# A two-layer decoder trunk: later convolution sums in the statistics bank, SiLU ordered behind the last exponential, state-space products as two of 64 stationary columns

## The chip, the cores and the metric

The kernel runs on one core of a Trainium2 chip, as a single launch. A core has five engines that matter here: TensorE (PE in the profile; its weight loads are shown apart as PEld), VectorE (DVE), ScalarE (ACT), GpSimd (POOL), and SyncE (SP), which only issues transfers. Each engine runs its own instructions strictly in its own order, and they wait for one another through semaphores. The metric is the device time of one execution in microseconds (us). The kernel before took 1105.08 us as the median of three runs (1103.52 to 1105.93).

## The reference, cut to what matters

The input is 512 positions of 1,024 channels, in float32. Two layers follow each other, each a mixer and then a gated feed-forward network (FFN), all with a residual add. The parts that the change touches are in the mixers:

```python
def conv_attn_mixer(xn, ...):                      # layer 0
    h = xn @ w_in
    glu_a, glu_g, c_q, c_kv, k_r = jnp.split(h, SPLIT_EVEN, axis=-1)
    u = glu_a * jax.nn.sigmoid(glu_g)              # 512 channels
    u = causal_dwconv(u, conv_w, conv_b)           # 31 taps, each channel alone
    u = jax.nn.silu(layer_norm(u, conv_ln_g, conv_ln_b))
    ...                                            # q, k, v of 8 heads from c_q, c_kv, k_r
    p = jax.nn.softmax(scores, axis=-1)            # blocks of 128 queries, causal
    attn = jnp.einsum('bhqk,bkhd->bqhd', p, v)     # 64 values per head
    return jnp.concatenate([u, attn], axis=-1) @ w_out

def s5_mixer(xn, ...):                             # layer 1
    u = (xn @ w_in).reshape(b, s, 32, 16)          # 32 groups of 16 channels
    bu = u projected on 64 complex states per group
    x = associative_scan(lam, bu)                  # complex diagonal recurrence in time
    y = Re(C x) + d_skip * u
    z = gelu(y) @ w_glu + b_glu
    return z[..., :1024] * jax.nn.sigmoid(z[..., 1024:])
```

The FFN is `silu(conv3(x @ w_up)[:2816]) * conv3(x @ w_up)[2816:]`, and then `@ w_down`. A last RMSNorm closes the trunk.

## The kernel before, in words

**Layout.** Channels lie on the 128 partitions and the 512 positions are the moving columns. A dense product is made of matmuls with a 128x128 stationary block and 512 moving columns. Weights and inputs are split into a rounded part and a remainder (`whi`, `wlo`; `xh`, `xl`), so that each dense product is three fast matmuls: the rounded weights come from a cast on ACT (L119), their remainders from subtractions on POOL (L121). Products that are left in plain float32 (scores, transposes, the values, the state-space tables) are matmuls without such a split.

**PSUM.** There are eight banks of 128x512, in four tags: three `sc`, two `pt`, two `b`, one `st`. `st` is for statistics (column means, sums of squares, their spreading over partitions).

**Layer 0.** After the input projection come the GLU, then two streams that are interleaved. The causal convolution has four blocks of 128 channels (`conv_gen`, L401 on): a block's sum `acc` stands in a PSUM bank of tag `pt`; DVE adds 20 or so taps to it (L405), while POOL adds the last 10, 10, 11 and 11 taps of the blocks into a sum of its own (L397), from products that ACT makes (L396). At the end ACT copies and DVE adds both into `ycv` (L411, L412), and the bank is free. The attention runs over 32 units (8 heads by 4 query blocks of 128). A unit's score (L553, and the mask added by L554) goes to an `sc` bank, DVE takes the row maximum (L556), ACT the exponential with its sum (L558), DVE the reciprocal (L559), POOL scales the row (L560); TensorE transposes it in 1 to 4 blocks into a `pt` bank (L567), and ACT copies that to SBUF (L570, `prob`). There are six buffers for scaled rows, and six units lie between a score and its transposes in the program. After each second head TensorE multiplies with the values (L583, two heads as two column halves of 64 in a `b` bank); ACT and DVE split the result (L587, L588). Behind the attention stands the LayerNorm of the convolution: mean (L615), squares (L620), `stat` and `spread`, scaling on DVE (L627), SiLU on ACT (L628), cast on ACT (L630) and remainder on POOL (L631). Both halves go into the output projection `wo` (L104), which is added to `x` (L648).

**FFN of layer 0.** While it starts, DVE and POOL also make the tables of the state-space layer from small vectors (from L763 on); a MEMSET of `pr` starts that chain, in memory that the convolution's pool leaves when the last POOL remainder (L631) is done. The norm of the FFN's input (`xh` L267, `xl` L268) and the FFN's own elementwise work (L922, L925, L937) are on the same DVE queue.

**Layer 1.** The state-space mixer works on four sets q of 8 groups each. A step `E` multiplies the set's inputs with table E (`e`, 8 products of a 128x128 table and 64 moving columns), and DVE runs the recurrence on it (`xs`); a step `T` multiplies the inputs with table T into bank `y`, a step `O` adds the states times table O, and then a GELU and two transfers give the input of the output projection `gl`. A string sets the order of these by hand, and TensorE's instructions are held to it (`D` is a number of dense matmuls, a number behind a comma how many dense matmuls are laid between the products of a step, `t` a load of tables):

```python
PLAN = "D39 t1 E0,12 t2 E1,8 D10 T0 O0 t3 E2 T1 O1 E3 T3 T2 A1 O2,6 D12 O3"
```

**What sets the order.** Outside of this string and of the convolution's taps, which are held in program order, a list scheduler places the instructions on each engine from its own estimates of when operands and buffers are ready. ACT needs a table of functions for exponentials and another for SiLU; it loads one (`ACT_TABLE_LOAD`) wherever two neighbours in its order differ.

Of the kernel before, what the change touches and what calls it, by code (L numbers as in the profile page):

```python
# [13 lines left out]
AF = mybir.ActivationFunctionType  # L14
# [20 lines left out]
NC = T // CL  # L35
# [36 lines left out]
def trunk(ctx, tc, A, out):  # L72
# [14 lines left out]
    def bank(name, tag=None):  # L87
        if tag is None:
            tag = CYCLE[turn[0] % len(CYCLE)]
            turn[0] += 1  # L90
        return pp.tile([128, T], F32, tag=tag, bufs=TAGS[tag], name=name)
# [6 lines left out]


    held = tc.keep_in_program_order  # L100
    fixed = [False]

    def mm(*a, **kw):
# [58 lines left out]
    def col(name, i=0):  # L162
        return vec[:, VOFF[name] + i:VOFF[name] + i + 1]
# [186 lines left out]
    with tc.tile_pool(name="l0", bufs=1) as lp:  # L350
# [12 lines left out]
        y, ysum = {}, []  # L363
# [34 lines left out]
                yield  # L398

        def conv_gen(i, u):  # L400
            acc = bank("acc", "pt")  # L401
            s.activation(acc, u, AF.Identity, scale=col("cw", i * CK + CK - 1), bias=col("cb", i))
            first = CK - POOL_TAPS[i]
            for sh in range(1, first):
                held(v.scalar_tensor_tensor(acc[:, sh:], u[:, :T - sh], col("cw", i * CK + CK - 1 - sh),  # L405
                                           acc[:, sh:], ALU.mult, ALU.add))
                yield
            while len(pools) and pools[0][0] <= i:
                pool_taps(1)
            y[i] = ya = lp.tile([128, T], F32, tag="acc", bufs=4, name="ycv")  # L410
            s.copy(ya[:, :first], acc[:, :first])  # L411
            v.tensor_tensor(ya[:, first:], acc[:, first:], psum_[i][:, first:], ALU.add)  # L412
            if i == 1:
                ysum.append(lp.tile([128, T], F32, tag="ysum", name="ysum"))
                v.tensor_tensor(ysum[0], y[0], y[1], ALU.add)
            elif i > 1:
                v.tensor_tensor(ysum[0], ysum[0], y[i], ALU.add)
# [121 lines left out]
        def head_q(h):  # L539
# [5 lines left out]
            v.tensor_tensor(q, ps, tO if h % 2 else tE, ALU.mult)  # L545
            return q

        def score(qi, qk):
            q, k = qk
            L = 128 * (qi + 1)  # L550
            sl = slice(qi * 128, L)
            ps = bank("sc", "sc")
            pe.matmul(ps[:, :L], q[:, sl], k[:, :L], start=True, stop=False)  # L553
            pe.matmul(ps[:, sl], identb, maskb, start=False, stop=True)  # L554
            mx = lp.tile([128, 4], F32, tag="mx", bufs=6, name="mx")
            v.reduce_max(mx[:, 0:1], ps[:, :L], axis=mybir.AxisListType.X, negate=True)  # L556
            p = lp.tile([128, T], F32, tag="p", bufs=6, name="p")
            s.activation(p[:, :L], ps[:, :L], AF.Exp, bias=mx[:, 0:1], accum_out=mx[:, 1:2])  # L558
            v.reciprocal(mx[:, 2:3], mx[:, 1:2])  # L559
            g.tensor_scalar(p[:, :L], p[:, :L], mx[:, 2:3], 1.0, ALU.mult, ALU.mult)  # L560
            return p
# [63 lines left out]
        rl = spread(rowstat((sqs, CW, LN_EPS))[0], two=True)  # L625
        for i in range(4):
            v.tensor_tensor(y[i], y[i], rl, ALU.mult)  # L627
            s.activation(y[i], y[i], AF.Silu, scale=col("ln_g", i), bias=col("ln_b", i))  # L628
            h, l = xhi(), xlo()
            s.copy(h, y[i])  # L630
            g.tensor_tensor(l, y[i], h.bitcast(F32), ALU.subtract)  # L631
            mix[4 + i] = (h, l)
# [328 lines left out]
    tTs, tOs = [], []  # L961
# [26 lines left out]

    xs, ys = {}, []

    def s5_state(q, d):
        gq = slice(8 * q, 8 * q + 8)
        cf, sf = (t[:, gq].rearrange("p g c -> p (g c)") for t in (tC, tS))
        e1 = bank("e1", "sc" if q < 3 else "b")
        for i in gaps(d):
            mm(e1[:, i * NC:(i + 1) * NC], tE[:, 8 * q + i], rs[q][:, i], start=True, stop=True)
        za, zb, z = ztmp("za"), ztmp("zb"), ztmp("z")
        lo, hi = slice(0, 64), slice(64, 128)

        def swapped(dst, src, low):  # L1000
            v.tensor_tensor(dst[lo], src[hi], sf[hi], ALU.mult)
            g.tensor_tensor(dst[hi], low[lo], sf[lo], ALU.mult)

        s.copy(z[lo], e1[lo])
        v.tensor_tensor(za, e1, cf, ALU.mult)
        swapped(zb, e1, z)
        v.tensor_tensor(za, za, zb, ALU.subtract)
        v.tensor_tensor_scan(z, tD[:, gq].rearrange("p g c -> p (g c)"), za, 0.0, ALU.mult, ALU.add)
        x_, xb = ztmp("xs"), ztmp("xb")
        xs[q] = as_g(x_)  # L1010
        g.memset(xs[q][:, :, 0:1], 0.0)
        v.tensor_tensor(za, z, cf, ALU.mult)
        swapped(xb, z, z)
        v.tensor_tensor(xs[q][:, :, 1:], as_g(za)[:, :, :NC - 1], as_g(xb)[:, :, :NC - 1], ALU.add)
# [3 lines left out]
    def s5_direct(q, d):  # L1018
        y = yb[q] = bank("y", "pt")
        for i in gaps(d):  # L1020
            mm(y[:, i * NC:(i + 1) * NC], tTs[q][:, i], rs[q][:, i], start=(i == 0), stop=False)

    def s5_out(q, d):
        y = yb[q]
        for i in gaps(d):
            mm(y[:, i * NC:(i + 1) * NC], tOs[q][:, i], xs[q][:, i], start=False, stop=(i == 7))
        ya = tmp("ya")
        s.activation(ya, y, AF.Gelu_apprx_tanh)
        dy = dp.tile([CL, 128, NC], F32, tag=f"dy{q}", name=f"dy{q}")
# [264 lines left out]
```

## Time and profile before

| | before |
|---|---|
| median of three runs | 1105.08 us |
| profiled execution | 1104.31 us, its span 1102.5 us |
| mean granted TensorE clock | 0.965 |
| TensorE busy | 1046.9 us (95%) |
| VectorE, ScalarE, GpSimd busy | 657.1, 454.0, 681.0 us |
| convolution taps and attention | about 100 to 190 us in the span |
| output projection `wo` | 175 to 226 us |
| FFN of layer 0 | from 226 us |
| state-space products | 640 to 687 us |

The times in the rows that follow are microseconds from the start of the span. A row of the timeline has the start, the busy time, the engine, the line and operation, the tile written and the tiles read, shapes, the number of instructions drawn together, and in square brackets how long the engine had been idle before it and what ended that. A row of the table by windows has, behind the window and its length, the busy time and number of instructions of PE, PEld, DVE, ACT and POOL, then the granted TensorE clock (1.00 is full), the share of the DMA engines and the GB/s. One float32 product of TensorE is recorded as two matmuls. The ends of matmuls are modelled, so lengths are read from one start to the next.

### The profile page before, as it was taken

The page shows a single profiled execution, that of the slowest core. Times are in us where ns is not written, and L with a number is a line of the kernel's source. Part 1 is how long each engine was busy: PE and PEld are TensorE (multiplying, and loading weights), DVE is VectorE, ACT ScalarE, POOL GpSimd, SP SyncE. Part 2 cuts the span into 40 slices and gives each one's busy share as a digit, 9 for nine tenths or more (in the row PEclk, how much of TensorE's full clock was granted, in tenths as well). Part 3 has the DMA queues.
Part 4 walks back from the last instruction along what each step waited for, and adds up shares of the span by engine and source line. Part 5 has one row for each costly group of instructions (what it writes and reads, how often), then busy time and mean ns, then how long its engine had stood idle before and what let it go on. Part 6 is the DMA issues. An engine that isn't in the chain of part 4 may idle for free.

```text
span 1102.5 us, 13795 instructions
## 1 busy us (share of the span) xinstructions
PE 1046.9 (95%) x4774; PEld 848.8 (77%) x4774; DVE 657.1 (60%) x1271; ACT 454.0 (41%) x669; POOL 681.0 (62%) x827
## 2 busy tenths in 40 slices
PE   7998698979999999999999799999999999999996
PEld 5875355857788878888888689788888888888896
DVE  7768871899865778547765465567531344314445
ACT  5567575341552253422444222544432344224441
POOL 4898841655677686766765652567656566556660
PEclk9999798989999999999999886999999999999998
DMA  5423010412233333333333552223223322232322
GB/s 189 144 68 90 14 40 1 130 64 91 78 114 113 116 104 110 115 103 109 97 101 110 210 153 60 91 84 110 98 93 107 102 98 96 77 115 96 101 73 77
DMA packets 54597, 108.64 MB, mean 99 GB/s; under 512 B 20608, under 2 KB 28416, under 8 KB 54528
## 3 DMA queue, kind: packets, MB, share of 16 engines
q1 hardware_dynamic: 54528, 107.77, 30.7%
q8 instruction: 38, 0.62, 0.2%
q14 instruction: 31, 0.25, 0.1%
HBM read 98.31 MB, written 8.39 MB: 97 GB/s over the span
## 4 chain that ended last, share of the span: by engine, by line
PE 77%; DVE 11%; ACT 5%; POOL 3%; issue 2%; DMA 2%; SPq 0%; DVEq 0%; ACTq 0%; POOLq 0%
PE dn L104 22%; PE ug L104 20%; PE ua L104 20%; PE gl L104 4%; POOL wlo L121 2%; PE y L104 2%; PE pv L583 1%; PE wo L104 1%; DVE acc L405 1%; PE w L104 1%; PE sc L553 1%; PE e L104 1%; POOL pa L397 1%; DMA raw<-w 1%; PE q L104 1%
## 5 line engine op out<-in xcount | busy, mean ns | idle before, releaser
L121 POOL TENSOR_TENSOR wlo<-raw,whi 128x256 fp32r<-128x256 f32 x639 | 486.2, 793 | 259.2 <-ACT whi L119 218.0
L119 ACT CAST whi<-raw 128x1024 fp32r<-128x1024 f32 (+1 forms) x162 | 167.2, 1037 | 303.1 <-PE dn L104 91.5
L104 PE MATMUL dn<-ghl,whi 128*128 128x512 f32 (+1 forms) x632 | 192.9, 387 | 0.0
L104 PE MATMUL ug<-xh,whi 128*128 128x512 f32 x352 | 138.6, 394 | 3.9 <-DVE wi L708 3.9
L104 PE MATMUL ua<-xl,whi 128*128 128x512 f32 x352 | 137.6, 391 | 4.2 <-DVE xl L268 4.2
L104 PE MATMUL ua<-xh,whi 128*128 128x512 f32 x352 | 138.0, 392 | 1.9 <-ACT xh L267 1.9
L104 PE MATMUL ug<-xh,wlo 128*128 128x512 f32 x352 | 138.2, 392 | 0.0
L104 PE MATMUL ug<-xl,whi 128*128 128x512 f32 x352 | 137.8, 392 | 0.0
L104 PE MATMUL ua<-xh,wlo 128*128 128x512 f32 x352 | 137.6, 391 | 0.0
L104 PEld LDWEIGHTS dn<-ghl,whi 128*128 128x128 f32 x632 | 117.3, 188 | 24.5 <-issue 0.8
L104 PE MATMUL dn<-ghl,wlo 128*128 128x512 f32 (+1 forms) x316 | 121.8, 386 | 0.0
L949 DVE TENSOR_TENSOR x<-x,dn 128x512 f32<-128x512 f32 x40 | 26.8, 683 | 110.0 <-PE dn L104 110.0
L925 DVE SCALAR_TENSOR_TENSOR ug<-h,vec,ug 128x511 f32<-128x511 f32 x88 | 66.3, 753 | 43.2 <-ACT ug L923 41.9
L925 DVE SCALAR_TENSOR_TENSOR ua<-h,vec,ua 128x511 f32<-128x511 f32 x88 | 66.3, 753 | 41.8 <-ACT ua L923 40.4
L104 PEld LDWEIGHTS ug<-xh,whi 128*128 128x128 f32 x352 | 66.8, 190 | 18.8 <-ACT whi L119 4.7
L104 PEld LDWEIGHTS ua<-xl,whi 128*128 128x128 f32 x352 | 66.3, 188 | 18.4 <-DVE xl L268 4.8
L104 PEld LDWEIGHTS ua<-xh,whi 128*128 128x128 f32 x352 | 66.4, 188 | 16.5 <-ACT xh L267 2.4
L104 PEld LDWEIGHTS ug<-xh,wlo 128*128 128x128 f32 x352 | 66.7, 190 | 14.2 <-POOL wlo L121 0.3
L104 PEld LDWEIGHTS ug<-xl,whi 128*128 128x128 f32 x352 | 66.7, 190 | 13.8
L104 PEld LDWEIGHTS ua<-xh,wlo 128*128 128x128 f32 x352 | 66.3, 188 | 14.0 <-POOL wlo L121 0.3
L941 POOL TENSOR_TENSOR ghl<-g,ghl 128x512 fp32r<-128x512 f32 x44 | 57.0, 1294 | 31.4 <-ACT ghl L940 31.4
L104 PEld LDWEIGHTS dn<-ghl,wlo 128*128 128x128 f32 x316 | 59.4, 188 | 11.8
(343 smaller groups left out, 1836.5 us busy)
## 6 DMA issues: line engine op xcount, KB each, us to landing
raw<-up SPq DMA_DIRECT2D x88, 512.0 KB, 3.3
raw<-down SPq DMA_DIRECT2D x32, 512.0 KB, 3.3
raw<-w SPq DMA_DIRECT2D x14, 512.0 KB, 3.5
raw<-down SPq DMA_DIRECT2D x16, 384.0 KB, 3.1
raw<-wg SPq DMA_DIRECT2D x8, 512.0 KB, 4.1
raw<-wo_a SPq DMA_DIRECT2D x4, 512.0 KB, 3.3
raw<-wo_c SPq DMA_DIRECT2D x4, 512.0 KB, 5.0
park_O<-wn SPq DMA_DIRECT2D x8, 256.0 KB, 2.6
```

Source lines behind the costliest of these rows:

```text
L104: r = pe.matmul(*a, **kw)
L119: s.copy(hi[:, :n], r)
L121: (eng or g).tensor_tensor(lo[:, a:a + 2], r[:, a:a + 2], hi[:, a:a + 2].bitcast(F32), ALU.subtract)
L397: held(g.tensor_tensor(pa[:, sh:], pa[:, sh:], pb[:, sh:], ALU.add))
L405: held(v.scalar_tensor_tensor(acc[:, sh:], u[:, :T - sh], col("cw", i * CK + CK - 1 - sh), acc[:, sh:], ALU.mult, ALU.add))
L553: pe.matmul(ps[:, :L], q[:, sl], k[:, :L], start=True, stop=False)
L583: pe.matmul(ps[a, kt * 128:], vv[:, kt, i * 128 + 64 * e:i * 128 + 64 * e + 64], pts[e][:, 4 * kt:3 * kt + 4].rearrange("p k c -> p (k c)" ...
L925: v.scalar_tensor_tensor(ps[:, sh:], t[:, :T - sh], col(fw, 3 * j + 2 - sh), ps[:, sh:], ALU.mult, ALU.add)
L941: g.tensor_tensor(lo, gt, h.bitcast(F32), ALU.subtract)
L949: v.tensor_tensor(x[m], x[m], ps, ALU.add)
```

## The change

There are three parts. The sums of convolution blocks 2 and 3 stand in the single `st` bank instead of the two `pt` banks, so block 3 begins when block 2 has left it, and the `pt` banks hold transposes alone from then on. The first SiLU is ordered behind the last exponential on ACT, with a dependency that is an order on one engine and no semaphore. Each product with a state-space table (24 per set: `e`, `y` from T, `y` from O) becomes two, with the first and the last 64 columns of the stationary block, written to the first and last 64 partitions of the same bank.

```diff
+    def behind(ins, first):
+        tc.add_manual_dep(ins.ins, first.ins.name, mybir.DependencyInfo(
+            mybir.DependencyClass.NoSync, mybir.DependencyReason.DATA), reason="order on one engine")
 ...
         def conv_gen(i, u):
-            acc = bank("acc", "pt")
+            acc = bank("acc", "pt" if i < 2 else "st")
 ...
+        exps = []
 ...
-            s.activation(p[:, :L], ps[:, :L], AF.Exp, bias=mx[:, 0:1], accum_out=mx[:, 1:2])
+            exps.append(s.activation(p[:, :L], ps[:, :L], AF.Exp, bias=mx[:, 0:1], accum_out=mx[:, 1:2]))
 ...
-            s.activation(y[i], y[i], AF.Silu, scale=col("ln_g", i), bias=col("ln_b", i))
+            silu = s.activation(y[i], y[i], AF.Silu, scale=col("ln_g", i), bias=col("ln_b", i))
+            if i == 0:
+                behind(silu, exps[-1])
 ...
+    def halves(ps, i, w, mv, start, stop):
+        for a in (slice(0, 64), slice(64, 128)):
+            mm(ps[a, i * NC:(i + 1) * NC], w[:, a], mv, start=start, stop=stop)
 ...
-            mm(e1[:, i * NC:(i + 1) * NC], tE[:, 8 * q + i], rs[q][:, i], start=True, stop=True)
+            halves(e1, i, tE[:, 8 * q + i], rs[q][:, i], True, True)
 ...
-            mm(y[:, i * NC:(i + 1) * NC], tTs[q][:, i], rs[q][:, i], start=(i == 0), stop=False)
+            halves(y, i, tTs[q][:, i], rs[q][:, i], i == 0, False)
 ...
-            mm(y[:, i * NC:(i + 1) * NC], tOs[q][:, i], xs[q][:, i], start=False, stop=(i == 7))
+            halves(y, i, tOs[q][:, i], xs[q][:, i], False, i == 7)
```

The scheduler's order moves with it. Line numbers below are those of each kernel: the change adds 5 lines ahead of the matmul helper (L104 becomes L109) and 7 ahead of the scores (L553 becomes L560).

TensorE, at the first transposes of the attention; before, nine scores stand ahead of the first transpose (`sc` is a score or its mask, `pt` a transpose of one block):

```order
L553 MATMUL sc<-kt,q 128x128
L554 LDWEIGHTS identb
L554 MATMUL sc<-maskb,identb 128x128
L567 MATMUL pt<-ident,p 128x128
L553 MATMUL sc<-kt,q 128x256
L554 LDWEIGHTS identb
L554 MATMUL sc<-maskb,identb 128x128
L567 MATMUL pt<-ident,p 128x128 x2
L553 MATMUL sc<-kt,q 128x384
```

The same engine and place in the changed kernel, from its second group of transposes on (the first transpose stands behind four scores):

```order
L560 MATMUL sc<-kt,q 128x128
L561 LDWEIGHTS identb
L561 MATMUL sc<-maskb,identb 128x128
L574 MATMUL pt<-ident,p 128x128 x5
L560 MATMUL sc<-kt,q 128x256
L561 LDWEIGHTS identb
L561 MATMUL sc<-maskb,identb 128x128
L574 MATMUL pt<-ident,p 128x128 x5
L560 MATMUL sc<-kt,q 128x384
```

Where one unit's transposes stood between two scores, those of two units do, since two `pt` banks take them; the column mean of the LayerNorm, which stood among the scores, now stands behind the last score.

ScalarE, around the SiLU of the LayerNorm, before (`p` is the exponential, `prob` the copy of transposes, `ycv` the SiLU in place):

```order
L628 ACT_TABLE_LOAD
L628 ACTIVATE ycv<-ycv,vec 128x512
L558 ACT_TABLE_LOAD
L558 ACTIVATE p,mx<-sc,mx 128x128
L570 COPY prob<-pt 128x3x128
L628 ACT_TABLE_LOAD
L628 ACTIVATE ycv<-ycv,vec 128x512 x3
L570 COPY prob<-pt 128x4x128
L558 ACT_TABLE_LOAD
L558 ACTIVATE p,mx<-sc,mx 128x256
```

And in the changed kernel (`whi` is the cast of a weight block of `wo`):

```order
L577 COPY prob<-pt 128x3x128
L577 COPY prob<-pt 128x4x128
L635 ACT_TABLE_LOAD
L635 ACTIVATE ycv<-ycv,vec 128x512 x2
L594 CAST xh<-pv 128x512
L639 CAST xh<-ycv 128x512
L635 ACTIVATE ycv<-ycv,vec 128x512
L639 CAST xh<-ycv 128x512
L635 ACTIVATE ycv<-ycv,vec 128x512
L639 CAST xh<-ycv 128x512
L124 CAST whi<-raw 128x1024
L639 CAST xh<-ycv 128x512
```

All four SiLUs now stand behind the last copy of transposes, with one table load ahead of them; the cast of a value product and one of weights stand among them. Over the whole kernel ACT's table loads go from 14 to 10.

TensorE, in the step E0, before (`w` is a dense matmul of the state-space input projection, `e` a product with table E):

```order
L104 MATMUL w_5822<-xl,whi 128x512
L104 MATMUL e_5847<-r,tabE 128x64
L104 MATMUL w_5822<-xh,wlo 128x512
L104 MATMUL e_5847<-r,tabE 128x64
L104 MATMUL w_5822<-xh,whi 128x512
```

And in the changed kernel:

```order
L109 MATMUL w_5822<-xl,whi 128x512
L109 MATMUL e_5847<-r,tabE 64x64 x2
L109 MATMUL w_5822<-xh,wlo 128x512
L109 MATMUL e_5847<-r,tabE 64x64 x2
L109 MATMUL w_5822<-xh,whi 128x512
```

The order around the products is the same; each product with a table is now two matmuls of 64 stationary columns, 192 in place of 96.

## The prediction

> **What bounds the kernel now.** I read the page's busy shares and chain first, then TensorE's timeline through the attention and the state-space products, then the other engines there.
>
> ```profile
> PE 1046.9 (95%) x4774; PEld 848.8 (77%) x4774; DVE 657.1 (60%) x1271; ACT 454.0 (41%) x669; POOL 681.0 (62%) x827
> PE 77%; DVE 11%; ACT 5%; POOL 3%; issue 2%; DMA 2%; SPq 0%; DVEq 0%; ACTq 0%; POOLq 0%
> ```
>
> TensorE sets the time. It can win only where it idles, where its clock is down, or where its own work shrinks. The attention has the first two:
>
> ```profile
> 111.01 0.44 PE L553 MATMUL sc<-kt,q 128*128 128x128 f32 x2
> 116.13 0.33 PE L567 MATMUL pt<-ident,p 128*128 128x128 f32 x1 [4.62 <-DVE ycv L412]
> 117.22 1.22 PE L553 MATMUL sc<-kt,q 128*128 128x256 f32 x2 [0.76 <-ACT p L558]
> ...
> 122.79 2.08 PE L553 MATMUL sc<-kt,q 128*128 128x512 f32 x2 [0.55 <-ACT p L558]
> ...
> 138.37 0.38 PE L553 MATMUL sc<-kt,q 128*128 128x128 f32 x2
> ...
> 159.70 0.38 PE L553 MATMUL sc<-kt,q 128*128 128x128 f32 x2
> ...
> 165.91 1.13 PE L553 MATMUL sc<-kt,q 128*128 128x512 f32 x2 [2.10 <-ACT p L558]
> ...
> 170.28 4.51 PE L583 MATMUL pv<-prob,vv 128*64 128x512 f32 x14 [3.07 <-ACT prob L570]
> ...
> 187.69 2.37 PE L583 MATMUL pv<-prob,vv 128*64 128x512 f32 x14
> 189.99 0.50 PE L104 MATMUL wo<-xh,whi 128*128 128x512 f32 x1
> ```
>
> The ninth of 32 scores starts at 111.01. The first transpose then waits 4.62 us for a convolution sum to leave its `pt` bank; both banks hold sums. From 117.22 to 122.79 two units pass, 2.8 us each; from 138.37, with the banks free, twelve units take 21.33 us, 1.78 each. The last score starts at 165.91, the last value product ends by 189.99. The windows show the clock falling with the idle time:
>
> ```profile
> 112.00:131.00 19.00, 12.04 (x30) 6.15 (x31) 16.55 (x31) 11.00 (x26) 16.62 (x17) 0.64 0.06 14
> 131.00:161.00 30.00, 28.35 (x150) 17.73 (x150) 24.21 (x66) 20.54 (x60) 13.97 (x23) 1.00 0.13 41
> 161.00:175.00 14.00, 8.83 (x36) 4.63 (x34) 4.52 (x13) 11.87 (x21) 2.86 (x6) 0.76 0.00 1
> ```
>
> The second hole, 161 to 175, is ACT's: 11.87 of 14 us busy, on copies, exponentials and table loads that alternate with SiLUs. Two of the four loads there:
>
> ```profile
> 166.25 1.28 ACT L628 ACT_TABLE_LOAD   x1
> ...
> 170.25 1.28 ACT L558 ACT_TABLE_LOAD   x1
> ```
>
> **The change, attention.** *Banks.* Transposes no longer wait for sums 2 and 3. From 111.01 I let the 23 other units run at 1.78 us: 40.9 us, so the last score starts near 152 instead of 165.91; I take 153. The work of the others fits, tightly: DVE was busy 16.55 + 24.21 = 40.8 us in the two windows up to 161, and some 7 of them (mean, squares and scaling of the LayerNorm) now stand behind the last score, which leaves 34 in 42 us. The new serial step, block 3's sum behind block 2's in one bank, costs nothing as long as DVE has other work and the mean is needed only behind the last score; if that cover is gone, the LayerNorm is late (third rival).
>
> *SiLU order.* No table load stands between exponentials. From the last score's start to the end of the last value product it was 189.99 - 165.91 = 24.1 us. Out of this fall the wait of 3.07 and the half clock on the product at 170.28 (4.51 against 2.37, so 2.1); the mean (1 us) comes in. 24.1 - 5.2 + 1.0 = 19.9, so 153 + 19.9 = 173, **17 us** earlier than 189.99. Below, the stretch from 138.37 to 159.70 also held LayerNorm matmuls that now stand elsewhere, about 2.5 us by an estimate; without them it is 1.57 per unit, 23 x 0.21 = 5 us less, an end at 168. Above, a quarter of a microsecond more per unit gives 179. That is a gain of 11 to 22.
>
> *What is late next.* The tail of the LayerNorm, and with it a chain on DVE:
>
> ```profile
> 190.58 2.18 ACT L630 CAST xh<-ycv 128x512 fp32r<-128x512 f32 x4
> 194.18 2.00 ACT L119 CAST whi<-raw 128x1024 fp32r<-128x1024 f32 x2 [1.42 <-PE wo L104]
> ```
>
> ```profile
> 191.29 5.05 POOL L631 TENSOR_TENSOR xl<-ycv,xh 128x512 fp32r<-128x512 f32 x4 [14.21 <-ACT xh L630]
> ```
>
> ```profile
> 196.42 0.09 DVE L763 MEMSET pr<- 128x32 f32 x1 [5.00 <-POOL xl L631]
> ...
> 270.65 0.68 DVE L922 TENSOR_TENSOR h<-ua,rb 128x512 f32<-128x512 f32 x1
> ```
>
> ```profile
> 237.86 0.79 PE L104 MATMUL ua<-xl,whi 128*128 128x512 f32 x1 [4.21 <-DVE xl L268]
> 277.46 0.79 PE L104 MATMUL ug<-xh,whi 128*128 128x512 f32 x1 [3.85 <-DVE wi L708]
> ```
>
> DVE starts its state-space tables at 196.42, 6.4 us behind the last value product, and works without a hole until `h` (270.65) empties the first bank of the FFN; TensorE waits for DVE at 237.86 and 277.46. So what lands is DVE's start, not TensorE's. In the changed order ACT's fourth `ycv` cast stands behind a cast of weights, which waits for the first block of `wo` (36 matmuls, as between 174.92 and 189.99, less what else lies there: some 4 us behind the value product), and POOL does four `wlo` pieces (about 0.8 us each, the 5.05 us above being 1.26 for each larger one) ahead of the last `xl`. Start behind the value product: 4.3 + 1.0 + 3.2 + 1.3 = 9.8 us instead of 6.4. DVE begins at 173 + 9.8 = 182.8, **13.6 us** earlier. Seven fewer small table instructions stand ahead of the first `h` in DVE's order; at some 0.27 us each 2 us more. The attention part lands at **-15.6 us**; bounds -22 (end at 168, tail as before) and -3 (third rival).
>
> **The change, state space.**
>
> ```profile
> 650.78 1.89 PE L104 MATMUL y<-r,tabT 128*128 128x64 f32 x16
> ...
> 659.07 3.62 PE L104 MATMUL y<-r,tabT 128*128 128x64 f32 x16
> 662.49 3.62 PE L104 MATMUL y<-xs,tabO 128*128 128x64 f32 x16
> ...
> 676.14 1.06 PE L104 MATMUL y<-xs,tabO 128*128 128x64 f32 x4
> ...
> 685.47 1.89 PE L104 MATMUL y<-xs,tabO 128*128 128x64 f32 x16
> ```
>
> ```profile
> 656.00:683.00 27.00, 27.00 (x120) 26.31 (x120) 20.09 (x21) 5.13 (x7) 9.72 (x9) 0.50 0.28 79
> ```
>
> A product takes (662.49 - 659.07)/8 = 0.427 us at half clock and some 0.225 at full. Weight loads are busy 26.31 of 27 us: the load of 128 float32 columns sets the pace, not the 64 moving columns. Whether two loads of 64 columns run beside each other, only the value products tell:
>
> ```profile
> 152.41 1.02 PE L553 MATMUL sc<-kt,q 128*128 128x512 f32 x2
> 153.27 0.22 PE L554 MATMUL sc<-maskb,identb 128*128 128x128 bf16 x1
> 153.42 2.37 PE L583 MATMUL pv<-prob,vv 128*64 128x512 f32 x14
> ```
>
> ```profile
> 181.19 1.07 PE L583 MATMUL pv<-prob,vv 128*64 128x512 f32 x2
> 182.19 0.50 PE L104 MATMUL wo<-xh,whi 128*128 128x512 f32 x1
> 182.53 0.39 PE L104 MATMUL wo<-xl,whi 128*128 128x512 f32 x1
> ```
>
> A float32 product of 512 columns takes 153.27 - 152.41 = 0.86 us. The 14 records at 187.69 are 2,048 columns in two halves; one after another they would take 3.4 us, and took 2.3. Halves do run beside each other, moving data at least. If loads do so too, a pair takes half a product: 0.213 at half clock. But one half alone, between other work (181.19 to 182.19), took 1.00 instead of 0.86, and the matmul behind it 0.34 instead of 0.23: a visit to the 64-column form costs 0.25 us.
>
> This drain is also a rule of the Trainium skill ("TensorEngine Tiling (Array Packing)", Key Properties: changing the tiling mode drains TensorE, and different tiles load and multiply in parallel); by its second half alone the stage would halve, by its first alone the 16 products of E0 and E1 would lose. The rows show both.
>
> Step by step. E0 and E1 stand between dense matmuls: 16 visits x 0.25 = 4 us more on TensorE; half of this shifts DVE's recurrence (2 us), since TensorE runs ahead of it. From then on DVE counts:
>
> ```profile
> 660.97 0.68 DVE L1014 TENSOR_TENSOR xs<-za,xb 128x504 f32<-128x504 f32 x1
> ...
> 667.52 0.68 DVE L1014 TENSOR_TENSOR xs<-za,xb 128x504 f32<-128x504 f32 x1
> ...
> 677.08 0.68 DVE L1014 TENSOR_TENSOR xs<-za,xb 128x504 f32<-128x504 f32 x1
> ```
>
> One set takes it 6.55 us, so the 40 products from 659.07 to 676.14, which would need 8.5 us instead of 17.1, cannot pass this on whole: `xs` of set 2 is ready at 670.2. Behind it stand O2, 18 dense matmuls (0.23 us each at full clock, 0.43 at half) and six visits: 6.5 to 12.4 us, and `xs` of set 3 comes at about 678.8. O3 starts between 678.8 and 682.6 instead of 685.47, so 3 to 6.7 us earlier; I take **-5 us**. Behind O3 the distance to the last `gl` parts stays. Bounds: -8 (no shift of DVE, clock up) and +5 (loads one after another, 0.45 us for a pair at full clock, next to the visits).
>
> **Sum.** 1104.31 (span 1102.5, 1.8 around it) - 15.6 - 5 = 1083.7; the median lies 0.8 above that execution: **1084 us**.
>
> **The rivals.**
>
> *Both parts pay, as above*: 0.53, about 1084, own range 1074 to 1091.
>
> *The state-space clock comes up too.* At 0.50 for 27 us with TensorE never idle, the rows speak against this; but the halves double the moving columns per time, and the sum would be at its bound, -8: 1081. Chance 0.07. "TensorE: Matmul & The Clock Gate" of the Trainium skill (Part 1) has the clock full after about 3.4 us of sustained work; by that rule alone the window above could not be at half clock, so the trace bears it out only if load-bound work doesn't count.
>
> *Halves don't overlap their loads.* The value products' 14 records have long moving parts that could hide serial loads, so this stands open: 0.225 stays 0.225 plus an issue cost, visits come on top, +5: 1104.31 - 15.6 + 5 + 0.8 = 1094.5. Chance 0.20.
>
> *The attention's gain is swallowed.* If block 3's sum ends so late that mean, squares, spread and SiLU follow far behind the last value product, DVE's tables start hardly earlier. With only 3 us left of 15.6: 1104.31 - 3 - 5 + 0.8 = 1097. For it speaks that POOL was busy 16.62 of 19 us while the taps ran. Chance 0.13, a quarter of it within no change.
>
> *Slower: the pace is not the banks'.* Score, maximum, exponential and scaling pass through DVE and POOL queues full of taps. If 2.8 us per unit is theirs, all 23 units cost 23 x 1.0 = 23.5 us more than I allow, and the result is 1084 + 23.5 = 1107.5. It decides from 1.78 + 21/23 = 2.7 us per unit. Against it: that stretch ran at clock 0.64 beside a single free bank, and DVE's share between 131 and 161, with taps until the mean, was still 24.21 of 30. Chance 0.07.
>
> **How the numbers follow.** A measurement of this kernel tells about 0.2% (2.2 us) from no change. Faster: 0.53 + 0.07 + 0.20 + 0.10 = 0.90; same 0.03; slower 0.07. The range takes the first four cases in: 1074 to 1098.
>
> **What would show it.** No wait for `ycv` ahead of the first transpose; the last value product ending near 173; DVE's MEMSET of `pr` near 183; no table load between exponentials. In layer 1, starts of successive products 0.11 or 0.21 us apart and O3 some 5 us closer to the start of E0. Wrong would be: units more than 2.4 us apart after 112, the MEMSET beyond 190, or products no closer than before.

## The result and the profile after

The changed kernel takes 1072.40 us (median of four runs, 1071.96 to 1073.62) beside 1105.51 us of the kernel before on the same chip (1103.52 to 1106.94): a ratio of 0.9708, with a 95% interval of 0.9687 to 0.9729, or 33 us less. 1084 were forecast, with 1074 to 1098 as the range; the result lies below it. The direction and both stages were right; the gain was half again as large. The profiled execution took 1072.81 us with a span of 1071.0 us, so the two spans differ by 31.5 us.

The page of the changed kernel, its busy shares and the chain:

```profile
PE 1025.4 (96%) x4966; PEld 826.2 (77%) x4966; DVE 660.5 (62%) x1271; ACT 447.5 (42%) x665; POOL 680.1 (63%) x827
...
PE 75%; DVE 15%; ACT 3%; DMA 2%; issue 2%; POOL 2%; SPq 0%; DVEq 0%; POOLq 0%; ACTq 0%
```

TensorE in the attention, from the timeline, and the windows of the same stretch:

```profile
106.57 0.27 PE L574 MATMUL pt<-ident,p 128*128 128x128 f32 x1
...
112.09 0.44 PE L560 MATMUL sc<-kt,q 128*128 128x128 f32 x2
...
148.29 1.08 PE L560 MATMUL sc<-kt,q 128*128 128x512 f32 x2
...
165.87 2.37 PE L590 MATMUL pv<-prob,vv 128*64 128x512 f32 x14
168.17 0.50 PE L109 MATMUL wo<-xh,whi 128*128 128x512 f32 x1
```

```profile
112.00:131.00 19.00, 17.95 (x95) 11.43 (x94) 17.75 (x40) 17.81 (x48) 17.79 (x24) 1.00 0.18 49
131.00:149.00 18.00, 18.00 (x94) 10.72 (x93) 15.54 (x42) 14.77 (x45) 16.15 (x23) 1.00 0.10 32
149.00:169.00 20.00, 20.00 (x104) 13.85 (x103) 12.05 (x33) 10.71 (x22) 2.12 (x3) 1.00 0.00 1
```

The first transpose no longer waits. From the ninth score (112.09) to the last (148.29) 23 units pass in 36.2 us, 1.57 us each; TensorE has work in 56 of the 57 us and the clock stays at 1.00, where it was at 0.64 and 0.76. From the last score's start to the end of the value products it is 168.17 - 148.29 = 19.9 us. They end 21.8 us earlier than before. From the ninth score on the gain is 22.9 us: the end of the value products lay 189.99 - 111.01 = 78.98 us behind it and lies 168.17 - 112.09 = 56.08 us behind it now. The other 1.1 us went in the first 100 us of this execution, where the order is the same and the first score came at 100.52 instead of 97.44. From the ninth score on the traces repeat well: 78.71 and 78.92 us in two further runs with the attention's order of before (halves alone, `nr` behind `xl` on before), 56.1 to 56.2 in all eleven others with the changed one.

What follows, on POOL and DVE, and TensorE's waits in the first FFN:

```profile
176.25 1.31 POOL L640 TENSOR_TENSOR xl<-ycv,xh 128x512 fp32r<-128x512 f32 x1
```

```profile
177.63 0.09 DVE L772 MEMSET pr<- 128x32 f32 x1 [8.05 <-POOL xl L640]
```

```profile
209.83 0.50 PE L109 MATMUL ua<-xl,whi 128*128 128x512 f32 x1 [1.93 <-DVE xl L273]
...
239.09 0.50 PE L109 MATMUL ug<-xh,whi 128*128 128x512 f32 x1 [2.76 <-ACT whi L124]
...
252.05 0.50 PE L109 MATMUL ug<-xh,whi 128*128 128x512 f32 x1 [1.43 <-ACT sl L943]
...
264.76 0.50 PE L109 MATMUL ug<-xh,whi 128*128 128x512 f32 x1 [1.47 <-ACT whi L124]
```

The first down-product (`dn`) of this FFN, before and in the changed kernel:

```profile
328.18 0.62 PE L104 MATMUL dn<-ghl,whi 128*128 128x512 f32 x2
```

```profile
303.30 0.62 PE L109 MATMUL dn<-ghl,whi 128*128 128x512 f32 x2
```

DVE's table work starts 9.5 us behind the last value product (6.4 before), 18.8 us earlier than before. The first down-product is 24.9 us earlier.

In the state-space layer, from the timelines of TensorE and DVE, and one window of the changed kernel, with the window of the kernel before behind it:

```profile
614.92 0.34 PE L109 MATMUL e<-r,tabE 128*64 128x64 f32 x4 [0.22 <-DMA r<-du]
615.19 0.50 PE L109 MATMUL w<-xh,wlo 128*128 128x512 f32 x1
615.62 0.34 PE L109 MATMUL e<-r,tabE 128*64 128x64 f32 x4
...
629.84 1.10 PE L109 MATMUL y<-xs,tabO 128*64 128x64 f32 x32
630.77 1.10 PE L109 MATMUL e<-r,tabE 128*64 128x64 f32 x32
...
638.40 1.98 PE L109 MATMUL y<-xs,tabO 128*64 128x64 f32 x32 [5.59 <-DVE xs L1027]
...
654.17 1.15 PE L109 MATMUL y<-xs,tabO 128*64 128x64 f32 x32 [1.56 <-DVE xs L1027]
```

```profile
637.02 1.33 DVE L1027 TENSOR_TENSOR xs<-za,xb 128x504 f32<-128x504 f32 x1
```

```profile
628.50:656.00 27.50, 19.69 (x343) 16.46 (x343) 24.82 (x24) 8.02 (x11) 13.87 (x13) 0.88 0.33 97
```

```profile
650.50:687.20 36.70, 35.42 (x181) 34.00 (x180) 25.49 (x26) 7.47 (x9) 13.81 (x14) 0.63 0.26 72
```

Eight pairs of halves take 630.77 - 629.84 = 0.93 us, 0.116 us for a product that took 0.225 at full clock and 0.427 at half. The clock in the stage is 0.88, where it was 0.63 over the stage and 0.50 in the 27 us without a gap; TensorE is busy for 19.69 of 27.5 us. TensorE now waits for DVE, 5.59 and 1.56 us. Behind the longer wait the clock is down again (0.50 from 638.4 to 642): eight pairs then take 640.16 - 638.40 = 1.76 us, 0.22 us each. From the last `gl` matmul on the shift is 31.9 us: 24.9 from the first layer and 7.0 from this stage.

### The profile page after: what moved, and what is told of

The parts are those of the page before. It is cut to its first block, busy times and chain, and to the rows that moved or that the text cites. A ratio compares the mean times of both kernels' runs of the same rounds, so it can differ in the third digit from the quotient of the medians.

```text
span 1071.0 us, 14173 instructions
## 1 busy us (share of the span) xinstructions
PE 1025.4 (96%) x4966; PEld 826.2 (77%) x4966; DVE 660.5 (62%) x1271; ACT 447.5 (42%) x665; POOL 680.1 (63%) x827
## 4 chain that ended last, share of the span: by engine, by line
PE 75%; DVE 15%; ACT 3%; DMA 2%; issue 2%; POOL 2%; SPq 0%; DVEq 0%; POOLq 0%; ACTq 0%
PE ug L109 20%; PE dn L109 20%; PE ua L109 20%; PE gl L109 4%; PE win L109 3%; POOL wlo L126 2%; DVE acc L410 2%; PE pv L590 1%; PE wo L109 1%; PE sc L560 1%; PE w L109 1%; PE pt L574 1%; PE kb L907 1%; DMA raw<-w 1%; ACT whi L124 1%
## 5 line engine op out<-in xcount | busy, mean ns | idle before, releaser
L109 PE MATMUL dn<-ghl,whi 128*128 128x512 f32 (+1 forms) x632 | 192.9, 387 | 0.0
L109 PE MATMUL ug<-xh,whi 128*128 128x512 f32 x352 | 138.0, 392 | 5.7 <-ACT whi L124 4.2
L109 PE MATMUL ua<-xl,whi 128*128 128x512 f32 x352 | 137.4, 390 | 1.9 <-DVE xl L273 1.9
L109 PE MATMUL ug<-xh,wlo 128*128 128x512 f32 x352 | 137.9, 392 | 0.2
L109 PE MATMUL ua<-xh,whi 128*128 128x512 f32 x352 | 137.6, 391 | 0.0
L109 PE MATMUL ug<-xl,whi 128*128 128x512 f32 x352 | 137.5, 391 | 0.0
L109 PE MATMUL ua<-xh,wlo 128*128 128x512 f32 x352 | 137.1, 390 | 0.0
L109 PEld LDWEIGHTS dn<-ghl,whi 128*128 128x128 f32 x632 | 117.3, 188 | 24.6 <-issue 0.8
L109 PE MATMUL dn<-ghl,wlo 128*128 128x512 f32 (+1 forms) x316 | 121.8, 386 | 0.0
L934 DVE SCALAR_TENSOR_TENSOR ug<-h,vec,ug 128x511 f32<-128x511 f32 x88 | 66.2, 753 | 42.7 <-ACT ug L932 41.4
L109 PEld LDWEIGHTS ug<-xh,whi 128*128 128x128 f32 x352 | 66.4, 189 | 20.9 <-ACT whi L124 5.1
L109 PEld LDWEIGHTS ua<-xl,whi 128*128 128x128 f32 x352 | 66.3, 188 | 16.0 <-DVE xl L273 2.4
L109 PEld LDWEIGHTS ug<-xh,wlo 128*128 128x128 f32 x352 | 66.2, 188 | 14.7 <-POOL wlo L126 1.1
L109 PEld LDWEIGHTS ua<-xh,whi 128*128 128x128 f32 x352 | 66.1, 188 | 14.2 <-issue 0.6
L109 PEld LDWEIGHTS ug<-xl,whi 128*128 128x128 f32 x352 | 66.3, 188 | 13.7
L109 PEld LDWEIGHTS ua<-xh,wlo 128*128 128x128 f32 x352 | 66.2, 188 | 13.8
L109 PEld LDWEIGHTS dn<-ghl,wlo 128*128 128x128 f32 x316 | 59.4, 188 | 11.7
```

Source lines behind the costliest of these rows:

```text
L109: r = pe.matmul(*a, **kw)
L934: v.scalar_tensor_tensor(ps[:, sh:], t[:, :T - sh], col(fw, 3 * j + 2 - sh), ps[:, sh:], ALU.mult, ALU.add)
```

## The experiments

Below, a shift is that of an instruction in the profiled execution against the same one in the profile before, whose own row shows where the two instructions stand. Each ratio is taken against the kernel before on the same chip and in the same hours; the runs come from several chips, so medians of different hours are compared by their ratios. The shift of the MEMSET of `pr` is DVE's start; "up-products" is the time from the last `wo` matmul to the first down-product of the first FFN, which is the same work for TensorE in every kernel.

| run | median, us | ratio to before (95%) | MEMSET of `pr` | first down-product | up-products |
|---|---|---|---|---|---|
| before | 1104 to 1106 | | 196.42 | 328.18 | 102.9 |
| changed | 1072.40 | 0.9708 (0.9687 to 0.9729) | -18.8 | -24.9 | 99.9 |
| bank alone | 1077.37 | 0.9755 (0.9718 to 0.9792) | -20.1 | -24.6 | 101.5 |
| SiLU alone | 1099.30 | 0.9946 (0.9920 to 0.9972) | -2.5 | -3.1 | 102.4 |
| halves alone | 1098.48 | 0.9943 (0.9928 to 0.9959) | -2.0 | -1.9 | 103.0 |
| whole in E0, E1, O2 | 1071.45 | 0.9701 (0.9666 to 0.9735) | -19.0 | -26.0 | 99.0 |
| changed, again | 1071.44 | 0.9687 (0.9662 to 0.9712) | -19.5 | -25.4 | 100.2 |
| last remainder on DVE | 1076.77 | 0.9744 (0.9725 to 0.9764) | -20.3 | -20.2 | 103.3 |
| block 3 alone in `st` | 1079.02 | 0.9759 (0.9740 to 0.9778) | -19.6 | -19.2 | 103.3 |
| shorter tables | 1071.00 | 0.9688 (0.9670 to 0.9706) | -20.0 | -25.9 | 100.2 |
| E0 and E1 in one run | 1069.00 | 0.9666 (0.9647 to 0.9685) | -20.6 | -27.2 | 99.3 |
| tables behind `xl` | 1078.81 | 0.9758 (0.9741 to 0.9774) | -19.1 | -21.0 | 104.0 |
| tables behind `rb` | 1081.36 | 0.9781 (0.9764 to 0.9798) | -21.8 | -23.9 | 103.9 |
| tables behind `rb`, E0 and E1 in one run | 1078.21 | 0.9746 (0.9724 to 0.9767) | -22.1 | -26.2 | 101.8 |
| `nr` behind `xl`, DVE remainder | 1078.34 | 0.9756 (0.9733 to 0.9778) | -25.2 | -21.6 | 106.9 |
| `nr` behind `xl`, before | 1107.71 | 1.0015 (0.9996 to 1.0035) | -0.3 | +2.7 | 105.9 |
| `pr` behind `xl`, DVE remainder | 1075.85 | 0.9726 (0.9705 to 0.9748) | -24.3 | -23.1 | 104.5 |

### The three parts alone

The bank alone, on the kernel before:

```diff
-            acc = bank("acc", "pt")
+            acc = bank("acc", "pt" if i < 2 else "st")
```

> The kernel before with the sums of blocks 2 and 3 in the statistics bank, nothing else. Its instructions stand on every engine in the same order as with the SiLU ordering added, 10 table loads included, so theory 1 (the bank alone makes the whole attention gain, the ordered SiLU adds nothing) expects what the changed kernel has without its state-space gain of 7.1 us: 24.9 us below before, 1080.6, and the last value product 21.8 us earlier. Theory 2 (the gain needs the ordered SiLU too, as the prediction put it) expects the wait of 3.07 us and the half clock at the last value products to be still there: 5 us less gain, 1085 to 1086.

It measured 1077.37 us, 27 us below the before of its hours (1104.33): theory 1. The last value product is 23.1 us earlier, 22.9 of them from the ninth score on. The order says why the ordered SiLU cannot add anything. In the traces of the bank alone and of the changed kernel TensorE, DVE, ACT and POOL have the same rows in the same order up to the state-space products, table loads included; the LayerNorm's mean stands behind the last score in both, so its SiLUs come behind the last exponential by themselves. The edit is inert in the changed kernel.

The ordered SiLU alone (`behind(silu, exps[-1])` for the first of the four):

> The kernel before with the first SiLU ordered behind the last exponential, nothing else. ACT's order here has 12 table loads instead of 14: the other three SiLUs, which are not ordered, still stand among the exponentials. Theory 1 (the bank is the cause): within 2 us of before, 1103 to 1106, with the wait of 4.62 us for the convolution sum unchanged. Theory 2 (the table loads cost what the second hole shows): 4 to 6 us faster, 1099 to 1101.

1099.30 us, 5.0 below before: the size that theory 2 gave, and theory 1's "within 2 us" was wrong. In its trace TensorE's and POOL's rows stand in the order of before, so that no matmul was moved. The profile shows the first hole untouched and the second one smaller:

```profile
117.30 0.33 PE L573 MATMUL pt<-ident,p 128*128 128x128 f32 x1 [4.63 <-DVE ycv L416]
...
168.23 3.79 PE L589 MATMUL pv<-prob,vv 128*64 128x512 f32 x14 [2.20 <-ACT prob L576]
```

So table loads among the exponentials did cost TensorE time: 3.07 became 2.20 us, 4.51 became 3.79, and the wait of 2.10 ahead of the last score went, 3.7 us in all with two of the four loads gone. But with the bank they go anyway, and the two gains are not two.

The halves alone:

> The kernel before with the state-space products as two of 64 columns, nothing else. Theory 1 (the stages add): 7.1 us below before, 1098.4, a pair of halves 0.12 us apart at full clock, and each product between dense matmuls 0.24 us dearer. Theory 2 (the gain of layer 1 depends on the earlier arrival, through transfers or table work of the first FFN): under 4 us, 1101 or more.

1098.48 us, 5.9 below before; in the traces the stretch from the first down-product to the last `gl` matmul is 5.2 us shorter (394.6 against 399.7 us). Nearer to theory 1, at a gain between the predicted 5 and the 7 of the changed kernel's trace. By the medians the bank's 27.0 us and the halves' 5.9 make 32.9, the 33 of the whole change; with the SiLU's 5.0 they would make 38.

### What bounds the state-space stage now

Whole products wherever dense matmuls lie between them:

```diff
-            halves(e1, i, tE[:, 8 * q + i], rs[q][:, i], True, True)
+            halves(e1, i, tE[:, 8 * q + i], rs[q][:, i], True, True) if not d else mm(e1[:, i * NC:(i + 1) * NC], tE[:, 8 * q + i], rs[q][:, i], start=True, stop=True)
```

(and the same in the O step.)

> The changed kernel, but the products of a step with dense matmuls between them (E0, E1, O2) stay whole, 128 columns; the steps without any keep their halves. Theory 1 (the 16 visits of E0 and E1 cost TensorE 0.24 us each and delay VectorE's recurrence): 2 to 4 us below the changed kernel, 1068.5 to 1070.5, and the wait for xs ahead of the second O step no longer than 5.6 us. Theory 2 (VectorE and GpSimd set this stage, TensorE waits for them anyway): within 1 us of the changed kernel, 1071.5 to 1073.5.

1071.45 us, no different from the changed kernel: theory 2. TensorE gets the visits back and hands them over to a wait:

```profile
636.98 1.97 PE L109 MATMUL y<-xs,tabO 128*64 128x64 f32 x32 [5.93 <-DVE xs L1027]
```

The products of E0 and E1 in one run each:

```diff
-PLAN = "D39 t1 E0,12 t2 E1,8 D10 T0 O0 t3 E2 T1 O1 E3 T3 T2 A1 O2,6 D12 O3"
+PLAN = "D39 t1 E0 D12 t2 E1 D18 T0 O0 t3 E2 T1 O1 E3 T3 T2 A1 O2,6 D12 O3"
```

> The changed kernel with the products of E0 and of E1 in one run each: 12 dense matmuls between the two steps and 18 behind E1, none between products. Theory 1 (VectorE's recurrence sets this stage, and an earlier E0 starts it earlier): no visits of 0.24 us, the recurrence begins some 4 us earlier, 2 to 4 us below the changed kernel's 1071.4. Theory 2 (GpSimd's weight remainders and VectorE's other work fill the stage anyway, as with whole products in E0 and E1): within 1 us.

1069.00 us, the lowest median of the study, with a ratio of 0.9666 where the changed kernel had 0.9708 and 0.9687; the interval overlaps that of the second (0.9647 to 0.9685, 0.9662 to 0.9712). The trace doesn't show a gain in the stage: from the first down-product to the last `gl` matmul it takes 392.1 us, 392.2 and 392.7 in the two profiles of the changed kernel. The 2 us stand in the first layer, which the edit doesn't touch. That fits theory 2. The same edit on the kernel with the tables behind `rb` (below) goes from 1081.36 to 1078.21 us on one chip, with intervals that just overlap; whether it is faster stays open.

### What sets the landing in the first FFN

The changed kernel again, as the reference of this part:

> The changed kernel itself, beside the three that differ from it in one place. All theories: 32 to 33 us below before, 1071 to 1073.

1071.44 us, as expected.

The fourth LayerNorm remainder on DVE instead of POOL:

```diff
-            g.tensor_tensor(l, y[i], h.bitcast(F32), ALU.subtract)
+            (v if i == 3 else g).tensor_tensor(l, y[i], h.bitcast(F32), ALU.subtract)
```

> The changed kernel with the fourth LayerNorm remainder (xl of ycv) on VectorE instead of GpSimd, where it stands behind four weight remainders. VectorE's table work should start 3 us earlier (near 174.6 instead of 177.6). Theory D (VectorE's start sets when the first FFN gets going): 2 to 3 us below the changed kernel. Theory T (TensorE lands by its own work; VectorE's chain only fills its waits): within 1 us of it.

Neither: 1076.77 us, 5.3 slower than the changed kernel of the same hours. DVE's start is 6.7 us behind the end of the value products (169.41 to 176.15) instead of 9.5 (168.17 to 177.63), so nearly 3 us earlier against TensorE, as meant, but the up-products take 103.3 us instead of 100. The scheduler laid the table work differently among the FFN's: the last remainder `xl` of the FFN's norm stands 144 rows of DVE behind the MEMSET of `pr` in this trace, not 118 as in the changed kernel's (138 and 115 in the count of the expectations).

The same position came with block 3's sum alone in `st`:

```diff
-            acc = bank("acc", "pt" if i < 2 else "st")
+            acc = bank("acc", "pt" if i < 3 else "st")
```

> The changed kernel with the sum of block 3 alone in the statistics bank; block 2 goes back to a pt bank, so that it holds one of two while blocks 2 and 3 are summed. If it is the number of free pt banks that sets the pace (theory 1), the units up to the end of block 2 run at a pace between 1.57 and 2.8 us; of the 27 us that the bank alone gave, a third to two thirds is lost: 9 to 18 us above the changed kernel. If one free bank is enough and only the full stop at the first transpose hurt (theory 2): at most 4 us above it.

1079.02 us, 7.6 above the changed kernel: less than theory 1 expected, more than theory 2. From the ninth score on the value products end after 60.7 us instead of 56.1 (79.0 before), and the up-products take 3 us longer. In the attention one free bank keeps the transposes going. Up to the last score (151.33) 5.4 us are lost: 1.0 us is the column mean, which stands among the scores again, and most of the rest lies in the one window whose clock is not full, with a wait of 2.58 us for DVE ahead of a projection:

```profile
112.00:131.00 19.00, 15.97 (x73) 9.88 (x72) 16.70 (x32) 14.28 (x39) 15.65 (x21) 0.91 0.15 41
```

So 18.3 of the 22.9 us come with one bank kept free, and the second bank is worth the smaller part. How much of the 18.3 is the full stop at the first transpose and how much the low clock behind it (0.64), these runs don't separate.

Shorter table work:

```diff
-        for j in range(CL):
-            v.tensor_copy(prr[:, j], pr[:, CL - 1 - j])
-            ts(spir[:, j], pi[:, CL - 1 - j], s1, None, ALU.mult)
+        v.tensor_copy(prr, pr[:, :CL])
+        ts(spir, pi[:, :CL], s1, None, ALU.mult)
```

> The changed kernel with two VectorE instructions in place of sixteen at the start of the table work: the powers are copied without reversing their order, which leaves the reversal out of the computation. Some 3.5 us of VectorE time go, seven instructions fewer stand ahead of the first h. Theory D (VectorE's chain sets the landing): 2 to 4 us below the changed kernel. Theory T (TensorE lands by its own work): within 1 us of it.

This kernel leaves out the reversal of the powers, so it computes other values; the rest of the program is the same. 1071.00 us against 1071.44: theory T. DVE's first `h` came at 242.62 instead of 248.20, which is 66.2 us behind the MEMSET of `pr` instead of 70.6 (this run, and the changed kernel):

```profile
242.62 0.68 DVE L930 TENSOR_TENSOR h<-ua,rb 128x512 f32<-128x512 f32 x1
```

```profile
248.20 0.68 DVE L931 TENSOR_TENSOR h<-ua,rb 128x512 f32<-128x512 f32 x1
```

TensorE waited for something else:

```profile
239.69 0.79 PE L109 MATMUL ug<-xh,whi 128*128 128x512 f32 x1 [5.75 <-ACT whi L124]
```

Then the table chain was ordered as a whole behind parts of the FFN's norm, with the helper of the change: behind the last `xl`, then with `norm_rb[-1]` in its place behind the norm's broadcast `rb`, then behind `rb` together with the single runs of E0 and E1:

```diff
-        ts(xc, a, -87.0, 88.0, ALU.max, ALU.min)
+        xc_ = ts(xc, a, -87.0, 88.0, ALU.max, ALU.min)
+        if a is ldt:
+            behind(xc_, norm_xl[-1])
```

(`norm_xl` collects the instructions that write `xl`, `norm_rb` those that write `rb`.)

> The changed kernel with the first instruction of the state-space table chain ordered on VectorE behind the last remainder xl of the first FFN's norm; that stands 34 instead of 115 instructions behind the MEMSET of pr. Theory X (of VectorE's chain only what stands ahead of these remainders and of the first h sets the landing): TensorE's waits for xl (1.9 us) and half of those behind it vanish, 3 to 6 us below the changed kernel, 1065.5 to 1068.5. Theory D (the length of VectorE's work from the MEMSET on sets it): within 1 us, since the same work is done.

> The same with the table chain ordered behind the whole norm of the first FFN (its scale rb); h then stands 49 instead of 203 instructions behind the MEMSET. Theory X: at least as early as with the order behind xl, all 8.3 us of waits and the half clock go, 6 to 9 us below the changed kernel, 1062.5 to 1065.5. Theory D: within 1 us. A wait that could come instead: the tables are late for the products of their own batch on TensorE (kb, ept), which would give some of it back.

> The order behind rb together with E0 and E1 in one run each. Theory 1 with theory X: the two gains add, 9 to 12 us below the changed kernel, 1059 to 1062.5. If E0 and E1 bring nothing: as the order behind rb alone.

All three were wrong by their sign: 1078.81, 1081.36 and 1078.21 us, by the ratios 4 to 10 us above the changed kernel (0.9708 and 0.9687). TensorE did run ahead at first (in the order behind `rb` the first third of the up-products has no wait), and then stood where the tables were late. TensorE and POOL of that run:

```profile
281.27 0.80 PE L109 MATMUL ug<-xh,wlo 128*128 128x512 f32 x1 [6.21 <-POOL wlo L126]
```

```profile
278.98 1.10 POOL L892 TENSOR_TENSOR e<-spir,bb 128x512 f32<-128x512 f32 x1 [2.03 <-DVE m L719]
280.04 3.79 POOL L126 TENSOR_TENSOR wlo<-raw,whi 128x256 fp32r<-128x256 f32 x4
```

POOL's order has weight remainders behind a product of the tables, which waits for DVE; TensorE waits for the remainder. The late tables were expected on TensorE's own table products and came through POOL's queue.

Last, the place of `xl` alone: one table instruction (`nr`, or one step earlier the first power `pr`) and what hangs on it ordered behind the last `xl`; the first and the third time on the kernel with the fourth remainder on DVE, the second time on the kernel before.

```diff
-        ts(nr, pr[:, 1], -1.0, None, ALU.add)
+        behind(ts(nr, pr[:, 1], -1.0, None, ALU.add), norm_xl[-1])
```

> Run q2 (fourth LayerNorm remainder on VectorE, 1076.8) with one table instruction (nr) and all that hangs on it ordered behind the last remainder xl of the first FFN's norm, which so stands 120 instead of 138 instructions behind the MEMSET of pr. If the place of xl makes the 6 us: 1070 to 1072.5, and the shift of the up-products is 5 to 7 us more than that of the MEMSET. If something else in q2's order makes them: 1075.5 to 1078.

> The kernel before with the same one order, and nothing else: the last xl stands 121 instead of 140 instructions behind the MEMSET of pr. If the place of xl makes the 6 us: 4 to 6 us below before. If it needs the earlier start too: within 2 us of before.

> As q11, with the order one step earlier in the chain (the first power pr): the last xl stands 92 instructions behind the MEMSET. If the tables stay early enough for GpSimd and ScalarE: as q11 or up to 2 us below it. If the trap of q8 and q9 begins here: 3 us or more above q11.

1078.34, 1107.71 and 1075.85 us. The last `xl` now stands 129, 129 and 98 rows behind the MEMSET. Its place alone does not make the difference: it brings nothing to the kernel before (ratio 1.0015, interval 0.9996 to 1.0035) and nothing to the run on which it was put (1078.34 us with it, 1076.77 without); one step earlier, 1075.85 us, the ratio is 0.9726 beside 0.9744, with overlapping intervals.

What these runs leave: the first down-product follows the last `wo` matmul by 99.0 to 101.5 us in six profiles of kernels that have the changed kernel's order there or nearly (the changed one twice, the bank alone, whole products, shorter tables, E0 and E1 in one run; all but the shorter tables have the very same order there, so these 2.5 us are the spread of one order), by 102.4 to 103.0 in the three with the places of before or nearly (before, SiLU alone, halves alone), and by 101.8 to 106.9 in the eight others. DVE's start spreads over 6.4 us among the kernels with the bank (171.2 to 177.6) and does not order them: the two earliest starts are in kernels with 104.5 and 106.9. How the scheduler lays the tables between the FFN's work on three queues moves the stretch by some 8 us. Which piece of that order gives the changed kernel its 3 us over before is not settled.

## Why the prediction was right or wrong

The sum missed 11 us on the profiled executions (-20.6 forecast, -31.5 measured): 9.3 in the attention part (-15.6 against -24.9) and 2.0 in the state-space part, less 0.4 that was lost again behind it. Most of it lies in two steps, and both missed in the same direction. The forecast's own terms give 1084.5 rather than 1084.

**Banks: right in mechanism, mis-sized by 4.8 us at the end of the value products (173 against 168.17), and by 5.9 from the ninth score on (17.0 against 22.9).** The wait for `ycv` is gone and the clock stays up. The term "23 other units at 1.78 us" failed: they took 1.57 us each, 36.2 us in place of the 42 between 111.01 and 153. With TensorE busy in 56 of 57 us at full clock that is its own work, not a pace of banks or of DVE. 1.57 is also the prediction's lower bound, which left out the LayerNorm's matmuls in the stretch of before, and that was the better reading; that it was met to the hundredth is luck. By the rows these matmuls took 2.0 us there and not the estimated 2.5, which gives 1.61, and the two stretches don't hold value products and projections in the same numbers. From the last score on, 19.9 us were forecast and 19.9 measured. The value products ended near 168, not 173.

**SiLU order: the effect right, the cause wrong.** No table load stands between exponentials, but the bank does that through the scheduler; the edit itself changes no row of any engine's order. Alone it gives 5.0 us by the medians, with an interval of 3 to 9, and 3.7 by the rows of its trace.

**"So what lands is DVE's start, not TensorE's": this step failed, by 4.4 us.** The tail was right (9.5 us against 9.8), so DVE started 3.0 us less early than TensorE's end had moved, as the step said (3.4). But that did not reach the end: from DVE's start to the first down-product it was 125.7 us instead of 131.8, where 2 us less were forecast for the seven fewer instructions. TensorE kept its whole 21.8 us and got 3.0 more out of the up-products, with 8.5 us idle in all instead of 10.0 and a clock of 0.98 instead of 0.95. Shortening DVE's chain brought nothing (`h` 4.3 us sooner behind the MEMSET, the same median), and starting it 2.7 us earlier against TensorE's end came with a slower kernel (1076.77); the chain of DVE was one of three queues there and not the bound. What made the up-products shorter by 3 us stays open.

**State space: right, 2 us short in the trace.** Loads of the two halves do run beside each other: 0.116 us for a pair against the 0.112 taken. A visit between dense matmuls costs 615.62 - 615.19 = 0.43 us for matmul and way back with 0.27 for the pair, 0.70 us in all; a whole product and its matmul took 641.68 - 641.23 = 0.45 us before. That is 0.25 us, as taken from one value product. O3 came 5.6 us closer to the start of E0 (39.25 us behind it instead of 44.80), against 5 forecast, and waited for `xs` there, as the step said; the 678.8 us that bounded it follow from no row shown, and on the same count it came at 679.9; its own halving (0.9 us) and a wait of 0.22 instead of 0.82 us for the inputs of E0, which were left out, make up the rest. The medians put the part at 5.0 to 5.9 us (changed against bank alone, halves alone against before).

That tiles load and multiply in parallel, and that a change of the tiling mode drains TensorE, as the Trainium skill has it ("TensorEngine Tiling (Array Packing)", Key Properties), agrees with both numbers. The rows of before held the cost of a visit and the parallel multiplying, but not the parallel loading, which the prediction left open with a chance of 0.20 against it; the 0.116 us show it.

**The rivals.** Clock up in the state-space stage: it did come up in the mean (0.88), though not behind the wait for `xs`, and was worth little, since TensorE waits there. Loads in series: refuted by 0.116 us. Gain swallowed by the LayerNorm's tail, and a pace set by DVE and POOL: refuted by the rows of the attention; DVE and POOL were 17.8 of 19 us busy there and kept up. The lower end of the range, 1074, stood on a bound of -22 us for the attention, with -24.9 measured: the bound took 168 for the end of the value products, which was right, but let everything behind it move by no more than that end.

## What to carry to other kernels

A PSUM bank that a long accumulation on VectorE holds can stop TensorE in a stage that seems unrelated; look at what the first wait for a bank does to the clock behind it. When a stage's pace is taken from a stretch of the old trace, take out the work that will no longer lie in that stretch, and test the rest against TensorE's own time. And before one engine's chain is said to set where a gain lands, look for the next waits on the other queues: taking that chain's cost away should move the end, and here it did not.

## What the runs showed of the hardware

Two 64-column halves of a float32 product with 64 moving columns are loaded and multiplied in 0.116 us at full clock, 32 matmul records in 0.93 us or 29 ns each, twice as fast as one of 128 columns (0.225 us); so this product, whose weight loads were busy for 26.31 of 27 us before, gains from column halves though all 128 columns are used. Products of this kind kept TensorE busy without a gap for 27 us at half the clock in the kernel before, so being busy alone did not bring the clock up here.

The first score of the attention began between 96.6 and 101.7 us in the thirteen profiled executions of kernels with the bank, whose instructions stand in the same order up to there; the waits and the clock of the first 97 us differ from one execution to the next (clock 0.95 in the changed kernel's trace, 0.98 in that with `nr` behind `xl`). Shifts of a few us between two single traces, counted from the start of the span, therefore say little; stretches that start at the ninth score repeat within 0.1 us wherever the order of the attention is the changed kernel's.
